# First-stage copies, banks and gates, latents in pairs, and two projections moved, in a one-core diffusion backbone

## The chip, the cores and the metric

The kernel runs on one core of one Trainium2 chip. The time is device microseconds (us) of one execution of the whole program. The core has a matrix engine (PE, TensorE), VectorE (DVE), ScalarE (ACT), GpSimd (POOL) and SyncE (SP), each with its own in-order queue. An instruction that waits holds up all that stand behind it on its engine. Results of PE go to PSUM, which has eight banks of 128 x 512 fp32. DMAs are issued here from SP's and from POOL's queue.

## The reference

One latent stream x (512 tokens, 1024 channels) goes through two layers. The change lies in the first: RMS norm with a shift and scale from the conditioning vector c (context tokens: from c_ctx), then multi-head latent attention over 256 context tokens and 512 latent ones.

```
m_lat = (silu_c @ ada_w[i] + ada_b[i]);  m_ctx = silu_cc @ ada_w[i] + ada_b[i]     # 6 x 1024 each
h_lat = rmsnorm(x, g) * (1 + sc_m) + sh_m          # h_ctx the same, from ctx and m_ctx
kv_a  = h @ wkv_a                                   # 256 latent + 64 rotary columns, 768 tokens
ckv   = rmsnorm(kv_a[..., :256]);  kv = ckv @ wkv_b # 8 heads, 128 key + 128 value columns
k     = rope(rmsnorm(concat(k_nope, k_pe)))
cq    = rmsnorm(h_lat @ wq_a)                       # 384 columns, 512 tokens
q     = rope(rmsnorm(cq @ wq_b))                    # 8 heads x 192
o     = softmax(q k^T * scale) v;  x = x + g_m * (o @ wo)
x     = x + g_f * (relu(modulate(x) @ w1) ** 2) @ w2
```

The second layer (gated mixing over positions, and another feed-forward) follows. Only the latent stream is returned.

## The kernel before

All data are fp32. A matrix product is made in three matmuls: each operand is split into a high part in fp32r and a low part that holds the rest, and high x high, high x low and low x high are added in PSUM (`mm3`, lines 80 to 82). The split of a weight is a cast on ScalarE (`split`, L72) and a subtraction on VectorE (L73), or with a scale L76. `Weights` loads a weight through SP's queue into one of four raw buffers and splits it; its high and low parts live in rings of five buffers in the first stage. A scheduler orders each engine's instructions by their place in the source, moved forward or back by what they need; `issue_after` puts an instruction behind another one of its engine.

The first stage has two pools of PSUM banks: `pt` with two and `pa` with six. It loads the tokens (`xn`), transposes them (`xct` for the context, `xt` for the latents) and spreads the inverse norms over partitions (`rp`, copied to `rsb`). Shift and scale of the first mixer come in four quarters of 256 channels. `ada_quarter(q)` loads four weights of 128 x 1024 (`ada<ch><q><i>`: ch 0 is the shift, 1 the scale), multiplies them with `c4` (silu of both conditioning vectors, high and low) in 32 matmuls into `ada_o`, copies the four rows to `adrow`, and turns them into columns `ada_c`, by matmuls with `sel`, which adds high and low. From the columns VectorE makes `bm` (shift) and `am` (scale). For each of eight channel tiles, `make_h` then forms `xa`, the high parts `ch`, `hh` on ScalarE and the low parts `cl`, `hl` on VectorE, and PE adds h times `wkv_a` into six accumulators `kva`, one for each tile of 128 tokens, which fill the six `pa` banks.

Behind that stand the latents. Each `kva` is normed (`kst`, with a power on GpSimd, L126), scaled to `ck`, transposed to `ckt` and split to `ckv_h`, `ckv_l`. In the same way `qa`, h times `wq_a` for one tile of tokens, becomes `cq`, `cqt`, `cq_h`, `cq_l`. `kv_proj(0)` makes keys and values of the first head, with a row of key norms `rkt`, `rr` that goes to DRAM and comes back over all partitions as `rk`. The rotary keys `krt` and `q_proj(0)` follow. In the attention `scores(h, half)` and `values(h, half)` go over eight heads in two halves of the tokens, with projections of later heads as fill between them. `scores` multiplies `s` by `rk` on VectorE (L638), so `rk` must be there.

In the background, `ada_step` makes the shifts, scales and gates of the other sublayers: GpSimd issues loads of `ada_w` (`adr`, 512 KB each, two buffers at first) and VectorE adds each to `acc`, eight to one row (L163, L165). These accs stand in VectorE's queue among the work of the latents.

## Time and profile before

| | us |
|---|---|
| median of 3 runs | 1386.79 (1385.57 to 1388.17) |
| profiled execution | 1386.22 |
| its span in the trace | 1384.4 |
| PE busy | 1335.3 (96%) |
| VectorE busy | 852.6 (62%) |
| ScalarE busy | 538.7 (39%) |
| GpSimd busy | 89.0 (6%) |

The span runs from the first to the last instruction of the trace; 1.8 us of the time lie around it. The mean clock granted to PE was 0.991 of full speed. The rows further down are from views of this one execution: a table of stretches of time, timelines of an engine (start, duration, engine, line, operation, output and inputs, shape, number, and in brackets how long the engine stood idle before and what ended that), groups of instructions, and DMA issues. A row with x12 stands for twelve instructions in succession.

### The profile page before, as it was taken

To read this page: it belongs to the slowest core of one execution; us is meant where nothing else is said; L and a number is where in the kernel's file an instruction comes from. 1 tells how busy PE (TensorE), PEld (TensorE's weight loads), DVE (VectorE), ACT (ScalarE), POOL (GpSimd) and SP (SyncE) were. 2 spreads that over 40 slices of the span, in tenths; PEclk is the share of its full clock that TensorE was granted. 3 is DMA by queue.
4 is the path that set the end of the run, shared out by engine and by line. 5 is a ranking of instruction groups with operands and counts; after the bars stand their busy time and mean duration, and the time that the engine had idled before them with its cause. 6 is when DMAs were issued, how large, how long until landed. Compare 5 with 4: busy or idle time off the path is not lost.

```text
span 1384.4 us, 18271 instructions
## 1 busy us (share of the span) xinstructions
PE 1335.3 (96%) x7071; PEld 1140.3 (82%) x7071; DVE 852.6 (62%) x1423; ACT 538.7 (39%) x1038; POOL 89.0 (6%) x140
## 2 busy tenths in 40 slices
PE   5988899999899999999999999999999999999998
PEld 4778889899888878888897888888888888888888
DVE  4877788887998888434466456555584344343452
ACT  6656556564641231422334323223254133241331
POOL 2031111110111111000000010000000000000000
PEclk8999999999999999999999999999999999999999
DMA  8551231321678886332323332222223223323311
GB/s 277 181 159 62 84 121 53 126 63 45 191 258 261 270 268 220 106 91 92 107 77 107 91 113 86 92 90 78 77 62 122 91 92 93 105 93 99 97 46 61
DMA packets 128070, 166.38 MB, mean 120 GB/s; under 512 B 7643, under 2 KB 111712, under 8 KB 127984
## 3 DMA queue, kind: packets, MB, share of 16 engines
q1 hardware_dynamic: 116032, 122.67, 28.1%
q0 software_dynamic: 11808, 42.03, 9.4%
q8 instruction: 55, 0.90, 0.3%
q10 hardware_dynamic: 144, 0.52, 0.1%
q14 instruction: 31, 0.25, 0.1%
HBM read 163.08 MB, written 2.12 MB: 119 GB/s over the span
## 4 chain that ended last, share of the span: by engine, by line
PE 78%; DVE 6%; DMA 5%; issue 5%; ACT 2%; POOL 1%; DVEq 0%; POOLq 0%; ACTq 0%
DMA adr<-in_ada_w_dram 5%; PE s L634 3%; PE v L80 2%; PE v L82 2%; PE v L81 2%; DVE acc L165 2%; PE f1d2o L80 1%; PE f1d0o L81 1%; PE f1d0o L82 1%; PE f1d0o L80 1%; PE f1d2o L81 1%; PE f1d2o L82 1%; PE f1d1o L80 1%; PE f0d2o L80 1%; PE f0d2o L81 1%
## 5 line engine op out<-in xcount | busy, mean ns | idle before, releaser
L165 DVE SCALAR_TENSOR_TENSOR acc<-adr,sil,acc 128x1024 f32<-128x1024 f32 x70 | 89.7, 1281 | 21.6 <-DMA adr<-in_ada_w_dram 21.4
L161 POOL DMA_DIRECT2D adr<-in_ada_w_dram x80 | 43.1, 539 | 223.9 <-DVE acc L165 129.5
L783 DVE TENSOR_TENSOR f1a<-f1a 128x512 f32<-128x512 f32 (+1 forms) x36 | 22.5, 629 | 38.1 <-ACT f1a L782 38.1
L72 ACT CAST f0uh<-f0a 128x512 fp32r<-128x512 f32 (+1 forms) x36 | 20.4, 572 | 53.3 <-DVE f0a L783 53.3
L638 DVE CUSTOM_DVE_ANT_0 p<-s,rk,rq 128x768 f32<-128x768 f32 x32 | 32.5, 1014 | 13.5 <-DMA rk<-rkd 9.2
L73 DVE TENSOR_TENSOR tl<-pt,th 128x512 fp32r<-128x512 f32 x48 | 32.0, 685 | 6.1 <-ACT th L72 5.9
L126 POOL TENSOR_TENSOR nst<-nst,mhalf 128x2 f32<-128x2 f32 x6 | 5.5, 919 | 455.9 <-DVE nst L125 455.9
L641 ACT ACTIVATE p<-p,sm 128x768 f32<-128x768 f32 x32 | 30.1, 941 | 12.1 <-DVE sm L640 12.1
L73 DVE TENSOR_TENSOR f1ul<-f1a,f1uh 128x512 fp32r<-128x512 f32 (+1 forms) x36 | 22.6, 632 | 19.7 <-ACT f1uh L72 19.5
L72 ACT CAST th<-pt 128x512 fp32r<-128x512 f32 x48 | 27.1, 587 | 18.8 <-PE o L82 12.6
L783 DVE TENSOR_TENSOR f0a<-f0a 128x512 f32<-128x512 f32 (+1 forms) x36 | 22.6, 627 | 18.1 <-ACT f0a L782 18.1
L72 ACT CAST f1uh<-f1a 128x512 fp32r<-128x512 f32 (+1 forms) x36 | 20.4, 572 | 32.8 <-DVE f1a L783 32.8
L73 DVE TENSOR_TENSOR f0ul<-f0a,f0uh 128x512 fp32r<-128x512 f32 (+1 forms) x36 | 22.5, 627 | 11.7 <-ACT f0uh L72 11.7
L80 PE MATMUL o<-th,vh 128*128 128x256 f32 x96 | 28.1, 293 | 0.7 <-ACT th L72 0.7
L81 PE MATMUL o<-tl,vh 128*128 128x256 f32 x96 | 28.3, 294 | 0.0
L601 DVE SCALAR_TENSOR_TENSOR xT<-wo,mod,xT 128x512 f32<-128x512 f32 (+1 forms) x40 | 25.1, 638 | 3.3 <-PE wo L82 3.0
L82 PE MATMUL o<-th,vl 128*128 128x256 f32 x96 | 27.1, 282 | 0.0
L656 PE MATMUL pt<-ident,p 128*128 128x128 f32 x192 | 26.8, 273 | 0.0
L893 DVE TENSOR_TENSOR gm<-gm,u 128x512 f32<-128x512 f32 x16 | 11.0, 689 | 20.6 <-ACT u L874 20.5
L656 PEld LDWEIGHTS pt<-ident,p 128*128 128x128 f32 x192 | 22.3, 141 | 1.0
L634 PE MATMUL s<-kh,qh 128*128 128x384 f32 x64 | 17.6, 357 | 4.3 <-DVE sm L638 4.2
L643 DVE TENSOR_SCALAR p<-p,sm 128x768 f32<-128x768 f32 x32 | 19.8, 618 | 0.6
(2637 smaller groups left out, 4622.8 us busy)
## 6 DMA issues: line engine op xcount, KB each, us to landing
adr<-in_ada_w_dram POOLq DMA_DIRECT2D x80, 512.0 KB, 4.8
rk<-rkd SPq DMA_DIRECT2D x8, 384.0 KB, 4.3
xn<-in_x_dram SPq DMA_DIRECT2D x4, 512.0 KB, 8.7
out_dram<-of SPq DMA_DIRECT2D x8, 256.0 KB, 2.1
xn<-in_ctx_dram SPq DMA_DIRECT2D x2, 512.0 KB, 3.6
ada000r<-in_ada_w_dram SPq DMA_DIRECT2D x1, 512.0 KB
ada001r<-in_ada_w_dram SPq DMA_DIRECT2D x1, 512.0 KB
ada100r<-in_ada_w_dram SPq DMA_DIRECT2D x1, 512.0 KB, 11.9
```

The source lines that it names most:

```text
L72: ACT.copy(out=hi, in_=src)
L73: eng.tensor_tensor(out=lo, in0=src, in1=hi.bitcast(F32), op=ALU.subtract)
L80: PE.matmul(o, lhsT=wh, rhs=mh, start=start, stop=False)
L81: PE.matmul(o, lhsT=wh, rhs=ml, start=False, stop=False)
L82: return PE.matmul(o, lhsT=wl, rhs=mh, start=False, stop=stop)
L161: nc.gpsimd.dma_start(out=r, in_=ada_w[l][k * P:(k + 1) * P, ch * D:(ch + 1) * D])
L165: DVE.scalar_tensor_tensor(out=acc, in0=r, scalar=sil[:, k, 0:1], in1=acc, op0=ALU.mult, op1=ALU.add)
L634: PE.matmul(S[:, n, :384], lhsT=a, rhs=b[:, n * 384:(n + 1) * 384], start=m == 0, stop=m == 4)
L638: DVE.tensor_tensor_reduce(out=e, in0=S[:, :, :384], in1=rk, op0=ALU.mult, op1=ALU.max, scale=rq, scalar=-3.0e38, accum_out=sm[:, 0:1])
L641: ACT.activation(out=e, in_=e, func=AF.Exp, bias=sm[:, 1:2], accum_out=sm[:, 2:3])
L656: PE.transpose(T[:, j, q * P:(q + 1) * P], Pr[h, 2 * half + q][:, (2 * jp + j) * P:(2 * jp + j + 1) * P], ident)
L783: DVE.tensor_tensor(out=f, in0=f, in1=f, op=ALU.mult)
```

## The change

In the first stage `t_c`, `t_cols` and `t_adab` take `pa` banks instead of `pt` banks, and the last two are issued behind the last transpose of x. The first quarter is written before `rp`, and `rp` is put behind its last matmul. One `adrow` copy takes both halves of `ada_o`. The columns come by four transposes, and a reduction on VectorE adds high and low (`adsum`). The scale half of a later quarter's splits is gated behind the `am` of the quarter before, and each quarter is written one ahead of its use, with the `wka` load first. The loads of cos, sin and of two gains stand behind the `wqa` loads in SP's queue. The latents go in pairs of token tiles: `ckv` in three, `cq` in two, with splits of 256 columns instead of 128. `query_latent(0)` is written before the norm of `kva`, in a `pt` bank. `kv_proj(1)` moves from behind the first scores into the latents.

```diff
-        t0 = pt("t_c")
+        t0 = pa("t_c")
-        t1 = pt("t_cols")
-        PE.transpose(t1[:, 16:87], rows, ident[:71, :71])
-        DVE.tensor_copy(out=cols[:, 16:87], in_=t1[:, 16:87])
-        t2 = pt("t_adab")
-        PE.transpose(t2[:, :96], arows, ident[:96, :96])
-        DVE.tensor_copy(out=adab, in_=t2[:, :96])
-        DVE.tensor_tensor(out=gqk, in0=cols[:, 53:54], in1=cols[:, 54:55], op=ALU.mult)
...
+        def ada_quarter(q, after=None, gate=None):
+
             row = inb.tile([4, 2, 256], F32, name="adrow", bufs=2)
             r = pt(f"ada_o{q}")
             for ch in range(2):
                 cs = slice(ch * 256, (ch + 1) * 256)
                 for i in range(2):
-                    wh, wl = W(ada_w[0], 4 * i, 4, ch * D + q * 256, 256, f"ada{ch}{q}{i}", POOL if SP[0] >> (2 * ch + i) & 1 else DVE)
+                    wh, wl = W(ada_w[0], 4 * i, 4, ch * D + q * 256, 256, f"ada{ch}{q}{i}", after=[gate] if gate and ch else ())
                     for k in range(4):
                         kk = 4 * i + k
-                        PE.matmul(r[:4, cs], lhsT=c4[:, kk, :], rhs=wh[:, k, :], start=kk == 0, stop=False)
-                        PE.matmul(r[:4, cs], lhsT=c4[:, kk, :], rhs=wl[:, k, :], start=False, stop=kk == KT - 1)
-                ACT.copy(out=row[:, ch, :], in_=r[:4, cs])
+                        with tc.issue_after(after) if after and kk == 0 else nullcontext():
+                            PE.matmul(r[:4, cs], lhsT=c4[:, kk, :], rhs=wh[:, k, :], start=kk == 0, stop=False)
+                        m = PE.matmul(r[:4, cs], lhsT=c4[:, kk, :], rhs=wl[:, k, :], start=False, stop=kk == KT - 1)
+            ACT.copy(out=row.rearrange("p c n -> p (c n)"), in_=r[:4, :])
+            o = pt(f"ada_c{q}")
             for ch in range(2):
                 for b in range(2):
-                    j = (2 * ch + b) * 2
-                    PE.matmul(o[:, j:j + 2], lhsT=row[:, ch, b * P:(b + 1) * P], rhs=sel, start=True, stop=True)
+                    j = (2 * ch + b) * 4
+                    PE.transpose(o[:, j:j + 4], row[:, ch, b * P:(b + 1) * P], ident[:4, :4])
             ks = slice(2 * q, 2 * q + 2)
-            o3 = o[:, :8].rearrange("p (c b j) -> p c b j", c=2, b=2)
+            sm = inb.tile([P, 4, 2], F32, name="adsum", bufs=2)
+            DVE.tensor_reduce(out=sm, in_=o[:, :16].rearrange("p (x s j) -> p x j s", x=4, s=2), axis=AX.X, op=ALU.add)
+            o3 = sm.rearrange("p (c b) j -> p c b j", c=2)
 
...
+            g = DVE.scalar_tensor_tensor(out=am[:, ks, :], in0=am[:, ks, :], scalar=1.0,
+                                         in1=bc(cols[:, G_MIX + 2 * q:G_MIX + 2 * q + 2]), op0=ALU.add, op1=ALU.mult)
+            return m.ins, g.ins
...
-                    PE.transpose(o[:, t * P:(t + 1) * P], xn[2 + t][:, k * P:(k + 1) * P], ident)
+                    last = PE.transpose(o[:, t * P:(t + 1) * P], xn[2 + t][:, k * P:(k + 1) * P], ident).ins
...
+        t1 = pa("t_cols")
+        with tc.issue_after(last):
+            PE.transpose(t1[:, 16:87], rows, ident[:71, :71])
+        DVE.tensor_copy(out=cols[:, 16:87], in_=t1[:, 16:87])
+        t2 = pa("t_adab")
+        with tc.issue_after(last):
+            PE.transpose(t2[:, :96], arows, ident[:96, :96])
+        DVE.tensor_copy(out=adab, in_=t2[:, :96])
+        DVE.tensor_tensor(out=gqk, in0=cols[:, 53:54], in1=cols[:, 54:55], op=ALU.mult)
+
+        m0, gate = ada_quarter(0, last)
         rp = [pa("rp0"), pa("rp1")]
         for t in range(NT):
             o = rp[0][:, t * P:(t + 1) * P] if t < 2 else rp[1][:, (t - 2) * P:(t - 1) * P]
-            PE.matmul(o, lhsT=rs6[:, t:t + 1].to_broadcast([P, P]), rhs=ident, start=True, stop=True)
+            with tc.issue_after(m0) if t == 0 else nullcontext():
+                PE.matmul(o, lhsT=rs6[:, t:t + 1].to_broadcast([P, P]), rhs=ident, start=True, stop=True)
...
             if k % 2 == 0:
-                ada_quarter(k // 2)
-                wkh, wkl = W(wkv_a, k, 2, 0, nka, f"wka{k}", POOL if SP[1] >> k & 1 else DVE)
+                wkh, wkl = W(wkv_a, k, 2, 0, nka, f"wka{k}")
+                if k < KT - 2:
+                    m0, gate = ada_quarter(k // 2 + 1, None, gate)
...
+        with tc.issue_after(bg_state["load"]):
+            nc.sync.dma_start(out=cosT, in_=rope_cos.rearrange("(t p) r -> p t r", p=P))
+            nc.sync.dma_start(out=sinT, in_=rope_sin.rearrange("(t p) r -> p t r", p=P))
+            nc.sync.dma_start(out=gq_b, in_=q_norm[:, NOPE:].to_broadcast([P, ROPE]))
+            nc.sync.dma_start(out=gk_b, in_=k_norm[:, NOPE:].to_broadcast([P, ROPE]))
...
-        for t in range(NT):
-            ck = wqp.tile([P, QL], F32, tag="ck", name="ck", bufs=3)[:, :KVL]
-            DVE.tensor_scalar(out=ck, in0=kva[t][:, :KVL], scalar1=st[:, 2:3], scalar2=None, op0=ALU.mult)
-            DVE.tensor_tensor(out=kg[:, t, :], in0=kva[t][:, KVL:nka], in1=gk_b, op=ALU.mult)
-            o = pt(f"ckt{t}")
-            for j in range(2):
-                PE.transpose(o[:, j * P:(j + 1) * P], ck[:, j * P:(j + 1) * P], ident)
...
-        kv0 = kv_proj(0)
-        for t in range(NL):
-            o = pa(f"qa{t}")
+        def query_latent(t):
+            o = qas[t] = (pa if t else pt)(f"qa{t}")
             for k in range(KT):
                 s = bass.ts(t, P)
                 mm3(o[:, :QL], hh[k][:, s], hl[k][:, s], wqa_h[:, k, :], wqa_l[:, k, :], k == 0, k == KT - 1)
-            if t >= QD:
-                latent_q(t - QD)
+            return o
+
+        query_latent(0)
+        for u in range(3):
+            st = ini.tile([P, 4, 2], F32, name="kst", bufs=3)
+            us = slice(2 * u, 2 * u + 2)
+            for j in range(2):
+                t = 2 * u + j
+                ACT.activation(out=junk[:, :KVL], in_=kva[t][:, :KVL], func=AF.Square, accum_out=st[:, 0, j:j + 1])
+                ACT.activation(out=junk[:, :ROPE], in_=kva[t][:, KVL:nka], func=AF.Square, accum_out=st[:, 1, j:j + 1])
+            rsq(st[:, 2, :], st[:, 0, :], 1.0 / KVL, EPS, st[:, 3, :])
+            DVE.tensor_scalar(out=epk[:, us], in0=st[:, 1, :], scalar1=1.0 / QK, scalar2=EPS, op0=ALU.mult, op1=ALU.add)
+            o = pt(f"ckt{u}").rearrange("p (k n) -> p k n", k=2)
+            for j in range(2):
+                t = 2 * u + j
+                ck = wqp.tile([P, QL], F32, tag="ck", name="ck", bufs=3)[:, :KVL]
+                DVE.tensor_scalar(out=ck, in0=kva[t][:, :KVL], scalar1=st[:, 2, j:j + 1], scalar2=None, op0=ALU.mult)
+                for k in range(2):
+                    PE.transpose(o[:, k, j * P:(j + 1) * P], ck[:, k * P:(k + 1) * P], ident)
+            s = slice(2 * u * P, (2 * u + 2) * P)
+            for k in range(2):
+                split(o[:, k, :], ckv_h[:, k, s], ckv_l[:, k, s], cols[:, G_KVA + k:G_KVA + k + 1])
+            for j in range(2):
+                DVE.tensor_tensor(out=kg[:, 2 * u + j, :], in0=kva[2 * u + j][:, KVL:nka], in1=gk_b, op=ALU.mult)
+        cqs = {}
+
+        def latent_q(u):
+
+            os_ = [pa(f"cqt{u}{i}").rearrange("p (k n) -> p k n", k=2) for i in range(2)]
+            for k in range(3):
+                for j in range(2):
+                    PE.transpose(os_[k // 2][:, k % 2, j * P:(j + 1) * P], cqs[2 * u + j][:, k * P:(k + 1) * P], ident)
+            s = slice(2 * u * P, (2 * u + 2) * P)
+            for k in range(3):
+                split(os_[k // 2][:, k % 2, :], cq_h[:, k, s], cq_l[:, k, s], cols[:, G_QA + k:G_QA + k + 1])
+
+        def rotary_keys(u):
+            o = pt(f"krt{u}")
+            for j in range(3):
+                PE.transpose(o[:, j * P:(j + 1) * P], kpe[:, 3 * u + j, :, :].rearrange("p a r -> p (a r)"), ident)
+            s = slice(u * 384, (u + 1) * 384)
+            ACT.copy(out=rh[:, s], in_=o[:, :384])
+            return DVE.tensor_tensor(out=rl[:, s], in0=o[:, :384], in1=rh[:, s].bitcast(F32), op=ALU.subtract).ins
+
+        kv0, kv1 = kv_proj(0), kv_proj(1)
+        ktmp = hp.tile([P, NT, ROPE], F32, tag="vl", bufs=3, name="ktmp")
+        for t in range(NL):
+            o = qas[t] if t in qas else query_latent(t)
             st = ini.tile([P, 4], F32, name="qst", bufs=4)
             ACT.activation(out=junk[:, :QL], in_=o[:, :QL], func=AF.Square, accum_out=st[:, 0:1])
             rsq(st[:, 2:3], st[:, 0:1], 1.0 / QL, EPS, st[:, 3:4])
             cqs[t] = wqp.tile([P, QL], F32, tag="ck", name="cq", bufs=3)
             DVE.tensor_scalar(out=cqs[t], in0=o[:, :QL], scalar1=st[:, 2:3], scalar2=None, op0=ALU.mult)
-        for t in range(NL - QD, NL):
-            if t >= KV:
+            if t == 1:
+                rope(DVE, kpe[:, :, 0:1, :], kg.unsqueeze(2), NT, 1, ktmp.unsqueeze(2), 0)
+                DVE.tensor_copy(out=kpe[:, :, 1, :], in_=kpe[:, :, 0, :])
                 drain(kv0, 1)
-            latent_q(t)
-        ktmp = hp.tile([P, NT, ROPE], F32, tag="vl", bufs=3, name="ktmp")
-        rope(DVE, kpe[:, :, 0:1, :], kg.unsqueeze(2), NT, 1, ktmp.unsqueeze(2), 0)
-        DVE.tensor_copy(out=kpe[:, :, 1, :], in_=kpe[:, :, 0, :])
-        for u in range(2):
-            o = pt(f"krt{u}")
-            for j in range(3):
-                PE.transpose(o[:, j * P:(j + 1) * P], kpe[:, 3 * u + j, :, :].rearrange("p a r -> p (a r)"), ident)
-            s = slice(u * 384, (u + 1) * 384)
-            ACT.copy(out=rh[:, s], in_=o[:, :384])
-            DVE.tensor_tensor(out=rl[:, s], in0=o[:, :384], in1=rh[:, s].bitcast(F32), op=ALU.subtract)
-
+            if t == 2:
+                latent_q(0)
+                drain(kv0, 1)
+        drain(kv0, 1)
+        rotary_keys(0)
+        rotary_keys(1)
+        drain(kv1, 1)
+        latent_q(1)
         drain(kv0)
+        drain(kv1)
 
 
 
@@ -692,7 +722,6 @@
...
         steps = [(h, half) for h in range(HEADS) for half in range(2)]
         scores(0, 0)
-        drain(kv_proj(1))
```

On PE, at the start of the first quarter, these rows stood after the last transpose of x (names: `rp` the spread norms, `t_cols` and `t_adab` the transposed gains and biases). Before:

```order
L428 MATMUL xt_259<-ident,xn_169 128x128
L436 MATMUL rp_266<-ident,rs_177 128x128 x2
L436 MATMUL rp_267<-ident,rs_177 128x128 x4
L366 MATMUL t_cols<-ident,rows 128x71
L369 MATMUL t_adab<-ident,arows 128x96
L389 MATMUL ada_o_278<-ada000h,c_82 4x256
L390 MATMUL ada_o_278<-ada000l,c_82 4x256
```

and after:

```order
L382 MATMUL ada_o_267<-ada000l,c_82 4x256
L381 MATMUL ada_o_267<-ada001h,c_82 4x256
L431 MATMUL t_cols<-ident,rows 128x71
L435 MATMUL t_adab<-ident,arows 128x96
L382 MATMUL ada_o_267<-ada001l,c_82 4x256
```

The quarter's matmuls now come first, with the two transposes among them. Its end, after the change:

```order
L381 MATMUL ada_o_267<-ada101h,c_82 4x256
L382 MATMUL ada_o_267<-ada101l,c_82 4x256
L444 MATMUL rp_335<-ident,rs_170 128x128 x2
L444 MATMUL rp_336<-ident,rs_170 128x128 x4
L388 MATMUL ada_c_325<-ident,adrow 128x4 x4
L381 MATMUL ada_o_352<-ada010h,c_82 4x256
```

`rp` has moved behind the whole quarter, and `ada_c` comes from transposes of `adrow`.

On VectorE, in the latents, where the accs and the latents share the queue. Before:

```order
L165 SCALAR_TENSOR_TENSOR acc_1351<-adr_1355,sil,acc_1351 128x1024
L125 TENSOR_SCALAR qst<-qst 128x1
L76 SCALAR_TENSOR_TENSOR ckv_l<-ckt_853,cols,ckv_h 128x128
L494 TENSOR_SCALAR ck<-kva_354,kst 128x256
L495 TENSOR_TENSOR kg<-kva_354,gk_b 128x64
L494 TENSOR_SCALAR ck<-kva_355,kst 128x256
L495 TENSOR_TENSOR kg<-kva_355,gk_b 128x64
L76 SCALAR_TENSOR_TENSOR ckv_l<-ckt_853,cols,ckv_h 128x128
L76 SCALAR_TENSOR_TENSOR ckv_l<-ckt_869,cols,ckv_h 128x128
L165 SCALAR_TENSOR_TENSOR acc_1351<-adr_1358,sil,acc_1351 128x1024
```

and after:

```order
L165 SCALAR_TENSOR_TENSOR acc_1405<-adr_1409,sil,acc_1405 128x1024
L125 TENSOR_SCALAR qst<-qst 128x1
L76 SCALAR_TENSOR_TENSOR ckv_l<-ckt_865,cols,ckv_h 128x256
L520 TENSOR_SCALAR ck<-kva_424,kst 128x256
L527 TENSOR_TENSOR kg<-kva_424,gk_b 128x64
L165 SCALAR_TENSOR_TENSOR acc_1405<-adr_1412,sil,acc_1405 128x1024
L125 TENSOR_SCALAR qst<-qst 128x1
L165 SCALAR_TENSOR_TENSOR acc_1405<-adr_1415,sil,acc_1405 128x1024
L520 TENSOR_SCALAR ck<-kva_425,kst 128x256
L527 TENSOR_TENSOR kg<-kva_425,gk_b 128x64
L556 TENSOR_SCALAR cq<-qa_830,qst 128x384
L76 SCALAR_TENSOR_TENSOR ckv_l<-ckt_888,cols,ckv_h 128x256
```

Between the `ck` of two neighbouring tiles now stand two accs where there was none, the first `cq` stands behind them (and behind one more acc ahead of these rows), and the splits have 256 columns.

On PE, at the end of the latents, before the first `q_proj(0)` matmul (`kt` are key transposes, `rkt` the key norms of a head). Before:

```order
L82 MATMUL kv_1165<-wkb0h,ckv_l 128x256
L535 MATMUL krt_1153<-ident,kpe 128x128 x3
L535 MATMUL krt_1159<-ident,kpe 128x128 x3
L266 MATMUL kt_1184<-ident,kn_1178 128x128 x2
L274 MATMUL rkt_1191<-ident,st_1079 6x128
L80 MATMUL q_1239<-wqb00h,cq_h 128x384
L81 MATMUL q_1239<-wqb00l,cq_h 128x384
```

and after:

```order
L82 MATMUL kv_1219<-wkb1h,ckv_l 128x256
L543 MATMUL krt_1134<-ident,kpe 128x128 x3
L266 MATMUL kt_1171<-ident,kn_1165 128x128 x2
L266 MATMUL kt_1171<-ident,kn_1209 128x128 x2
L274 MATMUL rkt_1190<-ident,st_982 6x128
L266 MATMUL kt_1238<-ident,kn_1232 128x128 x2
L274 MATMUL rkt_1245<-ident,st_1151 6x128
L80 MATMUL q_1293<-wqb00h,cq_h 128x384
L81 MATMUL q_1293<-wqb00l,cq_h 128x384
```

The second head's keys and values, with their `rkt`, now stand ahead of the query projection.

## Rows read from the trace of the kernel before

**Rows 1.** The page's busy times of the engines

```profile
PE 1335.3 (96%) x7071; PEld 1140.3 (82%) x7071; DVE 852.6 (62%) x1423; ACT 538.7 (39%) x1038; POOL 89.0 (6%) x140
```

**Rows 2.** Table of stretches: us, busy time (count) by engine, clock, DMA share, GB/s

```profile
0.00:22.80 22.80, 10.84 (x63) 8.45 (x64) 8.71 (x16) 16.60 (x28) 8.13 (x24) 1.00 0.88 284
22.80:74.70 51.90, 47.24 (x304) 37.84 (x304) 39.79 (x67) 28.66 (x47) 0.00 (x0) 0.90 0.59 182
74.70:112.20 37.50, 27.92 (x170) 26.36 (x170) 29.81 (x82) 20.33 (x80) 13.34 (x21) 0.95 0.53 165
112.20:200.00 87.80, 81.14 (x535) 75.97 (x536) 68.28 (x170) 53.96 (x165) 13.44 (x15) 0.98 0.29 89
200.00:1384.40 1184.40, 1168.14 (x6003) 991.66 (x6001) 706.02 (x1090) 419.17 (x720) 54.09 (x80) 1.00 0.36 115
```

**Rows 3.** PE's timeline of the first stage, start, us, instruction, idle before

```profile
22.82 0.33 PE L389 MATMUL ada_o<-ada000h,c 128*4 128x256 f32 x1 [4.25 <-DVE cols L367]
...
28.36 0.28 PE L389 MATMUL ada_o<-ada100h,c 128*4 128x256 f32 x1 [2.01 <-ACT adrow L391]
...
73.94 0.75 PE L82 MATMUL kva<-wka6h,hl 128*128 128x320 f32 x4
```

**Rows 4.** VectorE's timeline of the first stage

```profile
20.18 1.22 DVE L73 TENSOR_TENSOR ada100l<-ada100r,ada100h 128x1024 fp32r<-128x1024 f32 x1
...
33.49 0.48 DVE L447 SCALAR_TENSOR_TENSOR xa<-xcT,am,rsb 128x256 f32<-128x256 f32 x1
...
45.16 0.16 DVE L401 TENSOR_TENSOR bm<-ada_c,adab 128x4 f32<-128x4 f32 x1 [2.50 <-PE ada_c L395]
```

**Rows 5.** VectorE's busy time from first xa to last hl, one stretch

```profile
33.49:72.10 38.61, 33.51 (x56) 0.96 0.56 173
```

**Rows 6.** ScalarE's timeline of the first stage

```profile
27.00 1.04 ACT L72 CAST ada011h<-ada011r 128x1024 fp32r<-128x1024 f32 x1 [1.45 <-DMA ada011r<-in_ada_w_dram]
...
45.95 1.05 ACT L72 CAST ada121h<-ada121r 128x1024 fp32r<-128x1024 f32 x1 [4.49 <-PE kva L82]
```

**Rows 7.** PE's timeline of the latents, first ckt and first key norms

```profile
75.97 0.44 PE L498 MATMUL ckt<-ident,ck 128*128 128x128 f32 x2 [1.28 <-DVE ck L494]
...
112.16 0.38 PE L274 MATMUL rkt<-ident,st 128*6 128x128 f32 x1 [1.15 <-POOL st L272]
```

**Rows 8.** GpSimd's timeline, first background load after kva

```profile
75.62 1.17 POOL L161 DMA_DIRECT2D adr<-in_ada_w_dram  x2 [0.33 <-issue]
```

**Rows 9.** The page's DMA issues, the background loads

```profile
adr<-in_ada_w_dram POOLq DMA_DIRECT2D x80, 512.0 KB, 4.8
```

**Rows 10.** VectorE's timeline, last acc of the first eight

```profile
101.34 1.28 DVE L165 SCALAR_TENSOR_TENSOR acc<-adr,sil,acc 128x1024 f32<-128x1024 f32 x1 [1.00 <-DMA adr<-in_ada_w_dram]
```

**Rows 11.** VectorE's groups, 74.7 to 112.2: busy us, mean ns, idle before

```profile
L165 DVE SCALAR_TENSOR_TENSOR acc<-adr,sil,acc 128x1024 f32<-128x1024 f32 x7 | 9.0, 1283 | 5.4 <-DMA adr<-in_ada_w_dram 5.4
```

**Rows 12.** PE's timeline, head 1's projection and two rows of scores

```profile
126.21 0.28 PE L80 MATMUL kv<-wkb1h,ckv_h 128*128 128x256 f32 x1
...
127.63 0.58 PE L634 MATMUL s<-kh,qh 128*128 128x384 f32 x2
...
147.48 0.62 PE L634 MATMUL s<-kh,qh 128*128 128x384 f32 x2 [1.44 <-DVE sm L638]
```

**Rows 13.** VectorE's timeline, first softmax and second head's p

```profile
126.52 1.02 DVE L638 CUSTOM_DVE_ANT_0 p<-s,rk,rq 128x768 f32<-128x768 f32 x1 [0.42 <-PE s L634]
...
131.72 0.62 DVE L643 TENSOR_SCALAR p<-p,sm 128x768 f32<-128x768 f32 x1
...
146.40 1.02 DVE L638 CUSTOM_DVE_ANT_0 p<-s,rk,rq 128x768 f32<-128x768 f32 x1 [4.00 <-DMA rk<-rkd]
```

**Rows 14.** PE alone in one stretch: us, busy (count), clock, DMA share, GB/s

```profile
29.70:36.50 6.80, 6.56 (x31) 0.50 0.78 234
```

**Rows 15.** PE's timeline, transposes early and in the attention

```profile
6.51 2.82 PE L423 MATMUL xct<-ident,xn 128*128 128x128 f32 x12 [0.19 <-DMA xn<-in_ctx_dram]
...
139.85 1.04 PE L656 MATMUL pt<-ident,p 128*128 128x128 f32 x8
```

More of the change, by code (lines that the diff above doesn't have):

```diff
@@ L1 @@
-from contextlib import ExitStack, contextmanager
+from contextlib import ExitStack, contextmanager, nullcontext
 from types import SimpleNamespace
@@ L482, in hybrid_dit_kernel @@
         at.hp, at.W, at.pt, at.pm = hp, W, pt, pa
[L485 to L514 removed]
+        qas = {}
+        def query_latent(t):
+            o = qas[t] = (pa if t else pt)(f"qa{t}")
             for k in range(KT):
```

28 lines of the change are left out of this document (2 added, 26 removed).

## The prediction

> **What bounds the kernel now.** The page's list of engines comes first: PE is busy for 1335.3 of 1384.4 us [rows 1], so the end can only move by time in which PE stands still, or runs at the lower clock, or does less. The table by stretch tells where that is [rows 2]: span less PE's busy time is 12.0 us up to 22.8, 4.7 up to 74.7, 9.6 up to 112.2, 6.7 up to 200, and only 16.3 in the 1184.4 us behind. The change touches the first 160 us, so 32.9 us of standstill is what it can work on, and whatever it wins there arrives at the end unless the attention gives it back. The reader is then to see, in PE's timeline, two waits ahead of the first matrix's halves [rows 3], in VectorE's the operation from which the first stage is one long row of its work [rows 4, 5], in ScalarE's which load it stands for [rows 6], and behind the first stage a chain of loads that goes through VectorE's queue [rows 7 to 11].
>
> **The change part by part.** *First quarter, banks.* The first ada_o matmul starts at 22.82, 4.25 us after PE was ready, because cols' copy holds its bank and stands on VectorE behind four lo copies of 1.22 us; the second half waits 2.01 more for ScalarE to read the other half of the same bank [rows 3]. With t_c, t_cols and t_adab in the other pool, and one adrow copy for both halves, both waits have no reason left. The matmuls then follow the lo copies one by one, from about 18 us, and end soon after the last of them, near 24. But PE's gain of 5 to 6 us isn't the stage's: what opens the stage is the first xa on VectorE, at 33.49 [rows 4]. Ahead of it stand, in VectorE's new order, ada011l, a copy to rsb, the reduce, three small operations and ada110l; ada111l is now behind it. ada011l hangs on a load: ScalarE stood 1.45 us for ada011r, till 27.00 [rows 6], and its buffer had come free when ada100l ended, at 20.18 + 1.22 = 21.40 [rows 4], so 5.6 us passed between. The two rsb copies no longer stand ahead of ada100l, so it ends some 0.8 sooner: landing 26.2. Then 1.04 (hi), 1.22 (lo), about 0.7 for the copy of rsb (one and a half times xa's 0.48 [rows 4]), about 0.7 for the four small ones, 1.22 for ada110l: 31.1, less the overlap of neighbours, 30.5. If moving the four small loads off SP's queue brings ada011r 2 us sooner, it is 28.5; if the load takes 2 us longer, 32.5. I take **30.5, a lead of 3.0**.
>
> *From the first xa to the last hl.* That took 38.6 us, of which VectorE worked 33.5 [rows 5]. The change adds ada111l here (1.22) and three reduces. No row shows a reduce of this form; the nearest small one is 0.16, an upper end is 0.48 for 128x256 [rows 4]; I take 0.2 each, nearer the small one since it reads 16 columns. Sum 35.3. Of the 5.1 us of standstill, 2.50 is bm waiting for a quarter's columns [rows 4], which now come a quarter ahead; the 4.49 that ScalarE waits for wka0's buffer [rows 6] stays in part, since the extra weight load ahead only changes who asks for the buffer. I leave 1.5 us (0 to 5.1): 36.8. The last hl then ends at 67.3 instead of 72.1, **4.8 us sooner** (worst 32.5 + 40.4 = 72.9, best 28.5 + 35.2 = 63.7), and kva, which follows it [rows 3], near 69.9.
>
> *query_latent(0).* Its 24 matmuls of 384 columns move into this stage. At 0.118 us for 256 columns (12 kv matmuls between 126.21 and 127.63 [rows 12]) that is an estimate of 24 x 0.177 = 4.2 us. PE had 4.7 us idle in the stage [rows 2], and the stage begins earlier; it is hidden, and costs up to 4.2 if it isn't. It needs hh, hl and wqa, which come as the stage goes, and holds one of the two pt banks until its cq.
>
> *Pairs.* Twelve lo splits of 128 columns become six of 256, twice, and six rsq chains become three. In this stretch that makes VectorE's work a little less, while kv_proj(1)'s copies (vl three times, kl twice, wkb1l, some 3.3 us by the same operations later) come in; 29.8 of 37.5 us were busy [rows 2]. A pair's ck waits for two sums of squares and one pow, so the first ckt, which waited 1.28 us [rows 7], will wait about 3. I put the cost at nothing, because it isn't what ends last: adr loads do. The first is issued at 75.62, behind the last kva's pow [rows 8]; the last of its eight accs ends at 101.34 + 1.28 = 102.62 [rows 10]. That is 27.0 us with 5.4 us of VectorE waiting for the loads themselves [rows 11], each 4.8 us in flight [rows 9]. Then 9.5 us to the rkt transpose at 112.16 [rows 7], behind which q_proj begins. Nothing in the change shortens a load, so I move the chain as a whole: 70.8 + 27.0 + 9.5 = **107.3**, with the lead of 4.8 kept.
>
> *kv_proj(1).* Its 36 matmuls (36 x 0.118 = 4.2) and 7 transposes (0.1 each) leave the attention, where PE has no slack to speak of: 4.9 us. They enter a stretch where PE stands still for 9.6 us and which also loses 4.2 us of qa. Cover: these 13 us. So **4.9 us** come off, or nothing if the chain doesn't cover them.
>
> *Behind it.* VectorE waited 4.00 us and then PE 1.44 us for the second head's rk, a row that goes through DRAM [rows 12, 13]; its transpose now comes before q_proj, so 1.4 us go. On the other side kv1 stood between the first scores and the first value transposes, and covered the softmax: from 126.52 to the end of the first normalising at 132.3 are 5.8 us [rows 13], and what is left there (a third of kv_proj(2), four transposes of queries, the second scores) makes about 4.8 by its count; 1.0 us of new wait. Net **0.4**. The moved small loads of cos, sin and the two gains now land after wqa6 and are first needed by kg, behind ck: nothing, or if they come late something below the 4.00 us that rk's row costs now.
>
> **Sum**, against the profiled execution of 1386.2 us (span 1384.4, 1.8 around it; the median of the three runs is 0.6 above): 4.8 + 4.9 + 0.4 = 10.1, thus **1376**. The bounds of the first stage (-0.8 to 8.4), of query_latent (up to 4.2 lost) and of the last part (a loss of 1.0 to a gain of 1.4) make the range.
>
> **The rivals.** *PE becomes the bound of the first stage.* The granted clock was 0.50 in stretches behind the present waits, as from 29.70 to 36.50, where 31 matmuls took 6.56 us, twice their price [rows 14]. In the stage PE was busy 47.2 us; with qa's 4.2 it is 51.4 unless the waits' end also ends the low clock. In favour: twelve early transposes take 2.82 us, but eight later ones 1.04 [rows 15], and new transposes stand right ahead of the first quarter. Against: the stage's matmuls now follow each other sooner. If the clock stays low for ten more us, PE needs some 51 of the 52 us that it has, and the stage ends about 2 us later: **1378**, chance 0.12. The Trainium skill has a rule on this, in "TensorE: Matmul & The Clock Gate", section "Part 4: PE-mode transpose": the full clock doesn't engage for transposes. By that rule the case just priced would be the likely one; the early transposes agree with it and the later ones, at full pace, don't.
>
> *The attention takes filler back.* With kv1 gone, every later softmax could wait more. PE's 6.7 us of standstill from 112.2 to 200 [rows 2] is where it would grow. For: the order is otherwise the same from there, with a head's projection less in reserve. Against: fill work of heads 2 and 3 follows soon. At 4 us: **1380**, chance 0.14.
>
> *Slower: pairs behind the loads.* qa0 keeps a pt bank until its cq, and that cq and the later pairs' ck stand on VectorE behind up to four accs, each of which waits for a load of 4.8 us. If latents are served only link by link, q_proj's start is set by four serial links of issue 0.6, landing 4.8, acc 1.3 = 6.7 us. The end is later than now by more than 2.8 us only if q_proj starts beyond 112.2 + 5.3 + 2.8 = 120.3, that is 13.0 beyond my 107.3: four links 3.3 longer each, landings of 8.1 instead of 4.8. At that point **1389**, beyond it more. For: the DMA engines are already half busy there [rows 2], and wkb1's load joins. Against: the loads of the first 22.8 us moved 284 GB/s, here it was 165 [rows 2]. Chance 0.05.
>
> *The change doesn't reach the bound*, since ada011r or wka0's buffer sets the first stage as before and the lead is lost on VectorE, which is busiest from 112 on: 1386.2 - 1.4, about **1385**, chance 0.06. A first stage as good as its best bound gives **1370**, chance 0.07.
>
> **How the numbers follow.** My forecast has 0.56, between 1373 and 1378. The other gains (1378, 1380, 1370) have 0.33. About 0.2% or 2.8 us is what a measurement here can tell from no change: faster means below 1384.0. Faster is thus 0.56 + 0.33 = 0.89, less 0.01 for the upper tail of these: 0.88; same 0.07; slower 0.05. The range from 1370 to 1381 leaves out the last two rivals and half of the best case.
>
> **What would show it.** After: the first ada_o matmul near 18 rather than 22.82; first xa near 30.5; last kva near 70 with qa0's matmuls between; first ckt waiting about 3 us; eight accs still within about 27 us; q_proj from about 107; no wait for rk at the second head's p; standstill behind 200 us as before, 16. I am wrong if xa still starts past 33, if the accs' chain grows past 30, or if the waits for softmax in the first two heads grow by more than 2.

## The result, and the profile after

The changed kernel takes 1377.45 us (median of 4 runs, 1371.87 to 1378.22), the kernel before 1386.78. The ratio is 0.9932, with a 95% interval of 0.9910 to 0.9953: some 9.3 us sooner, where 1376 was forecast. The profiled execution is the fastest of the four (1371.87, span 1370.1), so one trace of it flatters the change by 5 to 6 us. A second trace of the same program, taken with the experiments (1377.59, span 1375.8), stands beside it below as *again*.

The table by stretch, in the same cuts as [rows 2], columns as there (behind the length: PE, its weight loads, VectorE, ScalarE, GpSimd):

```profile
0.00:22.80 22.80, 14.62 (x82) 11.33 (x83) 8.71 (x15) 16.60 (x28) 8.12 (x24) 0.93 0.83 278
22.80:74.70 51.90, 44.76 (x305) 38.44 (x303) 43.43 (x83) 34.30 (x67) 3.46 (x5) 0.95 0.71 218
74.70:112.20 37.50, 32.27 (x205) 30.85 (x203) 27.50 (x61) 19.40 (x74) 10.60 (x15) 0.89 0.48 145
112.20:200.00 87.80, 83.10 (x570) 78.55 (x569) 74.37 (x182) 55.37 (x164) 12.74 (x14) 1.00 0.28 86
200.00:1370.10 1170.10, 1155.64 (x5902) 978.82 (x5901) 696.40 (x1070) 410.80 (x693) 53.69 (x80) 1.00 0.36 116
```

PE stands still for 14.5 us behind 200 (16.3 before), so nearly all of the gain lies in the first 200 us, as forecast. PE's timeline of the first stage, which answers to [rows 3], and its end:

```profile
16.43 0.28 PE L381 MATMUL ada_o<-ada000h,c 128*4 128x256 f32 x1 [1.52 <-ACT ada000h L72]
17.69 0.28 PE L382 MATMUL ada_o<-ada000l,c 128*4 128x256 f32 x1 [0.98 <-DVE ada000l L73]
...
20.86 0.42 PE L381 MATMUL ada_o<-ada100h,c 128*4 128x256 f32 x1
...
68.33 0.75 PE L82 MATMUL kva<-wka6h,hl 128*128 128x320 f32 x4
```

Both waits of [rows 3] are gone; the first quarter's matmuls follow the copies one by one from 16.4. VectorE's timeline, which answers to [rows 4]: the small reduce, the first xa and the last hl,

```profile
28.28 0.17 DVE L391 TENSOR_REDUCE adsum<-ada_c 128x8 f32<-128x16 f32 x1
...
30.26 0.48 DVE L455 SCALAR_TENSOR_TENSOR xa<-xcT,am,rsb 128x256 f32<-128x256 f32 x1
...
64.25 0.75 DVE L457 SCALAR_TENSOR_TENSOR hl<-xa,bm,hh 128x512 fp32r<-128x512 f32 x1
```

and its busy time between them (columns as in [rows 5]):

```profile
30.26:65.00 34.74, 34.35 (x61) 0.98 0.73 216
```

VectorE now has 0.4 us of standstill there, where it had 5.1, so in this trace the first stage is VectorE's work almost alone. In *again* the same stretch is 36.6 us long with 2.2 of standstill, 2.1 of it waits for ScalarE's copies of `ada121` and `ada131`. Behind it, on PE, the first ckt and the start of q_proj ([rows 7]):

```profile
72.36 1.08 PE L522 MATMUL ckt<-ident,ck 128*128 128x128 f32 x4 [3.10 <-DVE ck L520]
...
106.53 0.38 PE L274 MATMUL rkt<-ident,st 128*6 128x128 f32 x1 [2.14 <-POOL st L272]
106.56 0.67 PE L80 MATMUL q<-wqb00h,cq_h 128*128 128x384 f32 x1
```

GpSimd's timeline has what I had not looked for, the first background loads ([rows 8]), and the power for which the last rkt waits:

```profile
63.45 1.16 POOL L161 DMA_DIRECT2D adr<-in_ada_w_dram  x2 [47.13 <-DVE cl L457]
...
105.15 1.33 POOL L272 TENSOR_TENSOR st<-st,mhalf 128x6 f32<-128x6 f32 x1 [4.53 <-DVE st L271]
```

Before, these two loads were issued at 75.62, behind the first power of kva's norm; now they stand ahead of it and go at 63.45. VectorE's eighth sum of the first row ([rows 10]):

```profile
94.07 1.27 DVE L165 SCALAR_TENSOR_TENSOR acc<-adr,sil,acc 128x1024 f32<-128x1024 f32 x1
```

So the chain is 31.9 us long (63.45 to 95.34), not 27.0, and ends 7.3 us sooner (in *again* 31.6 us and 5.2 sooner).

The best account is made from four landmarks on PE: the first ckt, the first q_proj matmul, the first matmul of the output projection (wo) and the first one with the second weight of the feed-forward (`f0u00w01h`, called f0 below; the first weight's matmuls start 6.3 to 7.1 us ahead of it in all runs). PE's busy time between them (us, busy with count, clock, DMA share, GB/s), before,

```profile
75.97:112.19 36.22, 27.91 (x169) 0.95 0.55 171
112.19:179.88 67.69, 62.55 (x419) 0.98 0.29 90
179.88:368.12 188.24, 181.15 (x1217) 0.98 0.28 90
```

and after, in the trace *again*:

```profile
74.22:108.61 34.39, 27.58 (x188) 0.98 0.52 155
108.61:168.47 59.86, 57.88 (x376) 0.96 0.29 90
168.47:359.94 191.47, 182.43 (x1216) 0.97 0.29 90
```

In the second trace the lead is 1.8 us at the first ckt, 3.6 at q_proj, 11.4 at wo, and 8.2 at f0, close to the 8.6 at the end. The first heads won 7.8, and 3.2 of that were given back behind them.

### The profile page after: what moved, and what is told of

It reads as the page before. It is cut to its first block, busy times and chain, and to the rows that moved or that the text cites. A ratio compares the mean times of both kernels' runs of the same rounds, so it can differ in the third digit from the quotient of the medians.

```text
span 1370.1 us, 18200 instructions
## 1 busy us (share of the span) xinstructions
PE 1330.4 (97%) x7055; PEld 1138.0 (83%) x7055; DVE 850.4 (62%) x1409; ACT 536.5 (39%) x1022; POOL 88.6 (6%) x137
## 4 chain that ended last, share of the span: by engine, by line
PE 85%; DVE 4%; issue 4%; DMA 3%; ACT 3%; POOL 0%; SPq 0%; DVEq 0%; ACTq 0%; POOLq 0%
PE s L664 3%; PE v L82 2%; PE v L80 2%; PE v L81 2%; DMA adr<-in_ada_w_dram 1%; PE f1d2o L80 1%; PE f1d0o L81 1%; PE f1d0o L80 1%; PE f1d0o L82 1%; PE f1d2o L81 1%; PE f1d2o L82 1%; PE f0d0o L80 1%; PE f0d1o L81 1%; PE f0d1o L80 1%; PE f0d1o L82 1%
## 5 line engine op out<-in xcount | busy, mean ns | idle before, releaser
L73 DVE TENSOR_TENSOR tl<-pt,th 128x512 fp32r<-128x512 f32 x48 | 31.9, 684 | 6.1 <-ACT th L72 5.8
L671 ACT ACTIVATE p<-p,sm 128x768 f32<-128x768 f32 x32 | 30.1, 941 | 13.3 <-DVE sm L670 13.3
## 6 DMA issues: line engine op xcount, KB each, us to landing
ada100r<-in_ada_w_dram SPq DMA_DIRECT2D x1, 512.0 KB, 11.4
```

The source lines that it names most:

```text
L73: eng.tensor_tensor(out=lo, in0=src, in1=hi.bitcast(F32), op=ALU.subtract)
L671: ACT.activation(out=e, in_=e, func=AF.Exp, bias=sm[:, 1:2], accum_out=sm[:, 2:3])
```

## The experiments

Each was timed in five rounds; the kernel before took 1385.3 to 1385.8 beside them. rk_late, no_adr, qa0_back and kv1_only ran on another chip than the other experiments; the kernel before took 1385.7 there, and 1385.75 and 1385.3 on the first chip. The table has the median, and from each one's trace the landmarks: start of the first ckt, and the lengths of the three stretches. Between the two traces of the changed kernel a length differs by up to 1.8 us and the start of the first ckt by 1.9.

| run | median us | first ckt | ckt to q_proj | q_proj to wo | wo to f0 |
|---|---|---|---|---|---|
| before | 1386.8 | 76.0 | 36.2 | 67.7 | 188.2 |
| changed (first trace) | 1377.5 | 72.4 | 34.2 | 59.2 | 189.7 |
| after_again | 1377.2 | 74.2 | 34.4 | 59.9 | 191.5 |
| first_old | 1382.4 | 78.7 | 34.2 | 60.2 | 191.5 |
| latents_old | 1379.6 | 71.8 | 36.0 | 68.1 | 188.9 |
| kv1_back | 1376.2 | 72.8 | 27.8 | 70.2 | 190.0 |
| kv1_only | 1384.8 | 76.5 | 41.4 | 59.4 | 191.5 |
| single_hoist | 1380.8 | 70.3 | 35.5 | 67.0 | 189.9 |
| qa0_back | 1378.0 | 74.3 | 35.9 | 59.9 | 192.1 |
| adr_behind | 1377.8 | 71.5 | 36.1 | 59.6 | 191.2 |
| no_adr | 1373.0 | 72.7 | 30.2 | 60.1 | 191.6 |
| before_no_adr | 1379.2 | 73.0 | 29.1 | 68.1 | 189.7 |
| rk_late | 1370.7 | 72.3 | 31.4 | 58.7 | 190.0 |
| adr_late | 1377.4 | 72.6 | 33.4 | 67.7 | 189.7 |

**after_again**, no edit.

> The changed kernel once more, unaltered, since its four times (1371.9, 1377.1, 1377.8, 1378.2 us) differ by more than those of before. If they come from two courses of one program, the profile and the times here fall at about 1372 or at 1377.5 with nothing between, and beside the first profile one place should show the 6 us. If it is a drift, they lie between.

Six runs gave 1374.63 to 1379.83, median 1377.17 (ratio 0.9934, 0.9917 to 0.9951). They lie between 1372 and 1377.5 and beyond: no two courses, but a spread. The two traces part step by step, 0.75 us at the first ada_c, 1.9 at the first ckt, 2.7 at wo, 4.4 at f0, 5.7 at the end. No single place holds it. The largest known part is VectorE's wait for two copies in the first stage, 2.1 us in the second trace and 0.2 in the first; what makes the rest was not settled.

**first_old and latents_old**, the two halves of the change: the first stage of before with the new latents, and the reverse.

The first, in the changed kernel, undoes all that stands ahead of `query_latent`:

```diff
-        t0 = pa("t_c")
+        t0 = pt("t_c")
...
-        m0, gate = ada_quarter(0, last)
...
-                if k < KT - 2:
-                    m0, gate = ada_quarter(k // 2 + 1, None, gate)
+                ada_quarter(k // 2)
...
```

> The first stage of before with the latents of the changed kernel (query_latent(0) ahead of kva's norm, pairs, the second head's projection moved). If the first stage's lead is passed on whole, this is 5 to 6 us slower than the changed kernel: the last hl near 72, q_proj near 112. Rival: the latents absorb it, as the background loads set their end and not the stage ahead of them; then it is less than 2 us slower.

The second undoes all from `query_latent` on:

```diff
-        query_latent(0)
-        for u in range(3):
+        for t in range(NT):
...
-        kv0, kv1 = kv_proj(0), kv_proj(1)
+        kv0 = kv_proj(0)
...
         scores(0, 0)
+        drain(kv_proj(1))
```

> The first stage of the changed kernel with the latents of before (single tiles, the first query matmuls behind the norms, the second head's projection behind the first scores). If the terms add, the end is 5 to 6 us sooner than before, and it and the run with the old first stage share the change's whole gain of 9 to 14 us between them. If the gain of one needs the other, both together fall short of it by 3 us or more.

With the old first stage the kernel takes 1382.38 (12 runs), 5.2 us more than the changed one, with the last hl at 72.3 and q_proj at 112.9, as expected. With the old latents it takes 1379.58, 6.2 us less than before. Thus the first stage brings 5 to 6 us and is passed on whole, and the rewritten latents bring 2 to 3.5 us. The halves add up (6.2 + 3.4 = 9.6 against 8.6).

**kv1_back and kv1_only**, the second head's projection put back, and moved alone.

In the changed kernel:

```diff
-        kv0, kv1 = kv_proj(0), kv_proj(1)
+        kv0 = kv_proj(0)
...
-        drain(kv1, 1)
...
-        drain(kv1)
...
         scores(0, 0)
+        drain(kv_proj(1))
```

> The changed kernel with the second head's projection back behind the first scores. If moving it gave 4.9 us of PE and the 1.4 us of rk's row, and if it cost nothing among the latents, this is 5 to 6 us slower than the changed kernel, with q_proj starting as early (106.6). Rival: the projection lengthens the latents, since its key norms stand ahead of q_proj on PE; then q_proj starts 3 to 4 us earlier here, near 103, and only about 2 us are lost at the end.

In the kernel before:

```diff
         drain(kv0)
+        drain(kv_proj(1))
...
         scores(0, 0)
-        drain(kv_proj(1))
```

> The kernel before with one edit, the second head's projection moved among the latents. If PE's standstill there (9.6 us) covers its 4.9 us, the end is 5 to 6 us sooner than before. If the projection's chain of splits, sums and power stands ahead of q_proj and delays it, q_proj starts some 3 us later and the end is 2 to 3 us sooner.

Putting it back costs nothing: 1376.22, 1.0 us below the changed kernel, within the spread. Moving it alone brings 1.0 us (1384.75, ratio 0.9993, 0.9979 to 1.0007), which the interval doesn't tell from nothing. The rival's mechanism holds in both, and is larger than was written: q_proj starts 6.0 to 8.0 us sooner with the projection put back, and 5.7 later with it moved alone. PE between the landmarks ckt, q_proj and wo, kv1_back first, then kv1_only:

```profile
72.75:100.58 27.83, 23.36 (x146) 0.96 0.61 182
100.58:170.80 70.22, 63.99 (x419) 0.94 0.29 86
```

```profile
76.46:117.85 41.39, 32.49 (x212) 0.97 0.52 163
117.85:177.23 59.38, 57.53 (x377) 0.96 0.27 86
```

Without the projection the new latents last 27.8 us, with it 34.4: it costs 6.6 there, and 5.2 in the old latents (36.2 to 41.4). In the heads it saves 10.4 and 8.3, of which 6.1 and 5.0 are PE's busy time and 4.3 and 3.3 its standstill. PE waited there behind the row of key norms, which is late where it follows the first scores (1.44 and 0.44 us before, 3.12 in kv1_back), and 1.9 us for the third head's power. VectorE's timeline of kv1_back:

```profile
135.67 1.02 DVE L666 CUSTOM_DVE_ANT_0 p<-s,rk,rq 128x768 f32<-128x768 f32 x1 [5.67 <-DMA rk<-rkd]
```

The standstill of the latents was not filled: in the old ones PE's busy time grew by 4.6 us and its standstill from 8.3 to 8.9, in the new ones by 4.2 and from 4.5 to 6.8. The projection makes new waits, as its tail stands ahead of q_proj on PE. PE's timeline of kv1_only, whose last rkt waits 3.08 us for the power on GpSimd while q_proj stands behind:

```profile
117.83 0.37 PE L274 MATMUL rkt<-ident,st 128*6 128x128 f32 x1 [3.08 <-POOL st L272]
117.85 0.67 PE L80 MATMUL q<-wqb00h,cq_h 128*128 128x384 f32 x1
```

**rk_late** moves that tail alone.

```diff
         drain(kv0)
-        drain(kv1)
+        drain(kv1, 2)
...
-        drain(q_proj(0)); ada_step(8)
+        drain(q_proj(0))
+        drain(kv1); ada_step(8)
```

> The changed kernel with the last step of the second head's projection, the transpose of its key norms and their way through DRAM, behind q_proj(0) instead of ahead of it. If PE's wait of 2.1 us for that power on GpSimd is what sets q_proj's start now, q_proj starts 2 to 3 us sooner, near 104, and the end is 2 to 3 us sooner than the changed kernel's. Rival: cq's low part or the query weights come at 106 anyway, or the second head's p then waits for rk; then nothing is gained.

It takes 1370.73 us (1367.86 to 1371.86; ratio to before 0.9888, 0.9868 to 0.9909), 6.4 less than after_again; the two intervals do not overlap, and so it beats both kernels. PE's timeline at the start of q_proj:

```profile
103.42 0.66 PE L266 MATMUL kt<-ident,kn 128*128 128x128 f32 x2 [0.88 <-ACT rr L276]
103.73 0.67 PE L80 MATMUL q<-wqb00h,cq_h 128*128 128x384 f32 x1
```

q_proj starts 2.8 us sooner than in the first trace of the changed kernel and 4.9 sooner than in the second; the wait of 2.1 to 2.4 for the power is gone, and the second head's p doesn't wait for rk. Against the second trace the landmarks show 3.0 of the gain in the latents, 1.2 in the heads and 1.5 behind them; 1.9 lies ahead of the first ckt, where the two programs don't differ, and belongs to the spread. So the moved tail is seen to bring some 3 us, as expected; for the rest of the 6.4 no cause was shown. The bulk of the projection, left in the latents, still costs 3.6 us there (31.4 against kv1_back's 27.8): PE's busy time is 5.0 longer, and only 1.4 of that came out of its standstill.

**single_hoist and qa0_back** part the pairs from the early query matmuls. single_hoist is latents_old with query_latent(0) alone moved ahead; qa0_back is the changed kernel with it moved back.

```diff
...
+        query_latent(0)
         kg = hp.tile([P, NT, ROPE], F32, tag="vh", bufs=3, name="kg")
...
```

> The run with the old latents (single tiles, the second head's projection behind the first scores, 1379.6 us), with query_latent(0) alone moved ahead of kva's norm. Beside kv1_back (1376.2, q_proj at 100.6) it lacks the pairs and what follows from them. If the pairs shorten the latents, q_proj starts at 104 or later. If the early query matmuls are what shortens them, q_proj starts near 101 and the end is within 1 us of kv1_back.

```diff
-            o = qas[t] = (pa if t else pt)(f"qa{t}")
+            o = qas[t] = pa(f"qa{t}")
...
-        query_latent(0)
```

> The changed kernel with query_latent(0) behind kva's norm, in a bank of the larger pool. Its 4.2 us of matmuls then leave the first stage, where they were said to be hidden. If the latents are bound by a chain and not by PE, nothing changes at the end (within 1 us), kva ends no earlier than 69 and the first wait for ckt grows. If PE's work binds the latents, q_proj starts up to 4 us later and so does the end.

Early query matmuls on single tiles bring nothing at the end (1380.75 against 1379.58). With pairs, undoing them costs 0.8 us at the end (1377.97) and 1.5 us in the latents, about the spread. But kv1_back, which differs from single_hoist by the pairs and by the order of the work that was written with them, has latents of 27.8 instead of 35.5 us and an end 4.5 us sooner. So the pairs, with that order, are what shortens the latents; the two were not parted. VectorE's busy time from the first ckt to q_proj shows how, kv1_back first, then single_hoist:

```profile
72.75:100.58 27.83, 24.09 (x57) 0.96 0.61 182
70.30:105.85 35.55, 29.50 (x79) 0.86 0.55 174
```

VectorE is busy for 5.4 us less, in 57 operations instead of 79 (2.3 us of it only moved out of the stretch: three splits of weights and one of the rotary keys), and stands still for 3.7 instead of 6.1. PE's timeline of single_hoist shows for what it waited, ckt after ckt:

```profile
81.65 0.44 PE L518 MATMUL ckt<-ident,ck 128*128 128x128 f32 x2 [2.29 <-DVE qst L125]
...
85.11 0.69 PE L518 MATMUL ckt<-ident,ck 128*128 128x128 f32 x2 [3.02 <-DVE ckv_l L76]
...
87.68 0.69 PE L518 MATMUL ckt<-ident,ck 128*128 128x128 f32 x2 [1.89 <-DVE cq L541]
```

VectorE's queue serves six tiles there; with pairs, only one later ckt waits, 0.7 us. These waits are not the length itself: latents_old has none of them and is as long (36.0), as PE does query matmuls in their place.

**no_adr, before_no_adr, adr_behind and adr_late** are on the background loads. The first two leave out seven of eight loads and sums of one row, from the changed kernel and from the kernel before.

```diff
-                nc.gpsimd.dma_start(out=r, in_=ada_w[l][k * P:(k + 1) * P, ch * D:(ch + 1) * D])
+                if n or not k:
+                    nc.gpsimd.dma_start(out=r, in_=ada_w[l][k * P:(k + 1) * P, ch * D:(ch + 1) * D])
+                if n == 0 and k:
+                    pass
-                if k == 0:
+                elif k == 0:
```

> The changed kernel without seven of the eight background loads and sums of the first row, which leaves that gate of the attention incomplete. By the prediction the chain of these loads sets the end of the latents: without it q_proj should start 8 us sooner or more, near 98. Rival: the latents are bound by PE, by the pairs' own chain and by the key norms ahead of q_proj; then q_proj starts 1 to 3 us sooner, no more than VectorE's freed 9 us let the copies come earlier.

> The kernel before without seven of the eight background loads and sums of the first row (that gate stays incomplete). The prediction moved the latents of before as a chain of these loads, 27.0 us plus 9.5 us behind. If that chain sets their end, q_proj starts 8 us sooner or more, near 104 instead of 112.2. Rival, as the same edit on the changed kernel showed: the loads are one burden of VectorE among others; q_proj starts 3 to 6 us sooner and the end is 3 to 5 us sooner.

adr_behind queues the loads behind the first power of kva's norm (`pw`) in the changed kernel:

```diff
...
-            rsq(st[:, 2, :], st[:, 0, :], 1.0 / KVL, EPS, st[:, 3, :])
+            pw = rsq(st[:, 2, :], st[:, 0, :], 1.0 / KVL, EPS, st[:, 3, :])
+            if u == 0:
+                bg_state["after"] = pw.ins
```

> The changed kernel with the first two background loads behind the first power of kva's norm on GpSimd, as in the kernel before, instead of ahead of it (they were issued at 63.5 us instead of 75.6). If the early issue is a gain of its own, the eight sums end some 4 us later and q_proj starts 1 to 4 us later, with the end as much later. If the sums don't bind, nothing changes within 1 us.

adr_late queues them in rk_late behind q_proj's last power (`at.pow`):

```diff
-            POOL.tensor_tensor(out=rq[:, us, :, 2], in0=rq[:, us, :, 1],
+            at.pow = POOL.tensor_tensor(out=rq[:, us, :, 2], in0=rq[:, us, :, 1],
...
-        drain(kv1); ada_step(8)
+        drain(kv1)
+        bg_state["after"] = at.pow.ins
+        ada_step(8)
```

> The version with the key norms behind q_proj (1370.7 us), and the background loads put behind q_proj's powers in GpSimd's queue, with all work done. If the loads only burden the latents, q_proj starts 3 to 4 us sooner than the 103.7 there and the end is 2 to 4 us sooner, near 1367.5. Rival: VectorE is as full behind q_proj (74 of 88 us) as among the latents, and the loads and sums slow the first heads by as much; then 1370 to 1373.

Without the row's loads the latents of before shrink by 7.1 us (36.2 to 29.1) and the end comes 6.1 sooner (1379.17); those of the changed kernel shrink by 4.0 to 4.2 (to 30.2), the end by 4.2 (1372.98). no_adr's q_proj comes 3.7 to 5.7 us sooner, between its two branches; before_no_adr's comes 10.1 sooner, but 3.0 of that lie ahead of the first ckt. So the loads with their sums did weigh on the latents of before, by most of the 8 us that the prediction's chain asks for, and weigh on them less now. The edit takes out VectorE's 9.0 us of sums together with the waits, so it doesn't tell a chain of loads from a burden of work. VectorE waits 2.5 us for the loads in the changed kernel where it waited 5.4 ([rows 11]); the same group after the change:

```profile
L165 DVE SCALAR_TENSOR_TENSOR acc<-adr,sil,acc 128x1024 f32<-128x1024 f32 x7 | 9.0, 1280 | 2.5 <-DMA adr<-in_ada_w_dram 2.5
```

Issuing the first two late again costs 1.8 us in the latents, where the sums then end 25.9 us behind the first ckt instead of 23.0 and 23.2, and 0.4 to 0.7 at the end (1377.84), which is within the spread. Putting them all behind q_proj is no gain: adr_late takes 1377.38, 6.6 more than the version that it started from and more than either branch had. PE's timeline in its first heads:

```profile
126.43 0.62 PE L664 MATMUL s<-kh,qh 128*128 128x384 f32 x2 [1.58 <-DVE sm L668]
130.45 1.01 PE L664 MATMUL s<-kh,qh 128*128 128x384 f32 x2 [1.25 <-DVE sm L668]
```

The sums now stand among the softmax's operations, and the stretch to wo lasts 67.7 us instead of 58.7. Its latents, with no loads in them, are not shorter (33.4 against 31.4). VectorE's busy time in them, and then PE's, show that the work of PE now fills them:

```profile
72.57:105.98 33.41, 20.11 (x59) 0.95 0.10 32
```

```profile
72.57:105.98 33.41, 28.78 (x188) 0.95 0.10 32
```

VectorE stands still for 13.3 us, 5.7 of it for ckt transposes on PE, and PE is busy for as long as in rk_late (28.8 against 28.4 us). So without the loads there was little left to win here; why the stretch is 2 us longer stays open.

## Why the prediction was right, and where it was not

**First stage: right.** The first xa came at 30.26 (30.73 *again*; 30.5 was said), the last hl ended at 65.0 and 67.3 (67.3 was said), the last kva group ends at 69.1 and 70.9 (near 70 was said). first_old prices it at 5.2 us against 4.8. Only the parts inside were a little off: VectorE's work was 34.4 in both rather than 35.3, and its standstill 0.4 and 2.2 rather than 1.5. The reduce took 0.17 us (0.2 was said).

**Latents: the right place by luck, from two errors of opposite sign.** q_proj was put at 107.3 and came at 106.6 and 108.6. But the step "I put the cost at nothing" for the pairs failed: with the order written with them they are a gain of 7.7 us in the latents (single_hoist to kv1_back), since fewer operations go through VectorE's queue. The loads, issued 12 us sooner, past the first power on GpSimd, have some 1.8 us of it (adr_behind). The chain of loads was not moved as a whole either: it grew to 31.9 and 31.6 us, past the 30 that was named as a sign of being wrong, and it no longer ends last, since 11.2 us lie between its end and q_proj instead of 9.5. I had taken the first load to follow "the last kva's pow"; the one ahead of it in [rows 8] was the first of six (at 74.73), and I had not looked at the new order of GpSimd's queue.

**kv_proj(1): the step that failed most.** Its "4.9 us come off, or nothing if the chain doesn't cover them" took the first branch. The runs show that in the latents it costs 5.2 (kv1_only) or 6.6 us (kv1_back), most of what the pairs had won. The sum of standstill, 9.6 us, was no cover: PE's standstill there did not shrink but grew, by 0.6 and 2.3 us. Of the 6.6 us, 3.0 go when the tail (PE to ScalarE to VectorE to GpSimd and back to PE) is moved behind q_proj, and 3.6 stay with the bulk (rk_late). Its gain in the heads was also mis-sized: 8.3 to 10.4 us instead of 4.9 + 0.4, with 3.3 to 4.3 us of standstill where I had taken the 1.44 of one wait. At the end it is worth 1.0 us alone, which the noise covers, and nothing in the changed kernel.

**The attention gives filler back: right as a rival, but not where it was put.** From wo to f0 every version with the projection moved takes 189.7 to 192.1 us and those with it in place 188.2 to 190.0. In *again* the loss is 3.2 us, where the rival had 4. The rival looked for it in PE's standstill from 112.2 to 200, and that fell, from 6.7 to 4.7 us in both traces. It is from wo to f0 that PE's standstill grew, from 7.1 to 9.0, and its busy time by 1.3; the waits for the softmax grew from 2.3 to 4.7. The largest of them on PE, before and then in *again*:

```profile
181.74 0.61 PE L634 MATMUL s<-kh,qh 128*128 128x384 f32 x2 [1.00 <-DVE sm L638]
```

```profile
172.05 1.01 PE L664 MATMUL s<-kh,qh 128*128 128x384 f32 x2 [2.68 <-DVE sm L668]
```

Of the 1.0 us of new wait that the forecast had at the first softmax little is there: PE's longest wait from 108.6 to 159.7 in *again* is one of 0.39 us.

**The other rivals.** PE did not become the bound of the first stage: the clock was low in two stretches of 3.4 and 3.3 us (below), and VectorE, with 0.4 us of standstill, did not wait for it. The serial links of the slower rival did not form, since q_proj started at 106.6 to 108.6, far from 120.3. The change did reach the bound of the first stage; the reason given for that rival, VectorE busiest from 112 on, misreads [rows 2], which has 81.14 us of PE there and 68.28 of VectorE. The first ckt's wait of 3.10 us was the 3 that was said, but it was not free: a lead of 5.6 us at kva's end became 3.6 at ckt.

Thus 10.1 us were forecast as 4.8 + 4.9 + 0.4. By place this came near: *again* has a lead of 3.6 us at q_proj (4.9 was said) and wins 4.6 from there to f0 (5.3 was said). By cause it did not: 5.2 us come from the first stage and 3.4 from the latents and heads together, in which pairs (a gain) and the projection (about nothing) have changed places.

## What to carry to other kernels

Standstill summed over a stretch is not room for more work: here 4.9 us of work filled none of 8.3 us in the old latents, and in the new ones, with its tail moved away, 1.4 of 4.5. Look at what the moved work's last instruction waits for, and at what stands behind it on that engine. When work is moved ahead of a stage, leave its last round trip behind the stage's first matmuls; here that was 3.0 us in the latents for a few lines, and the end came 6.4 sooner. And read the new order of every queue, GpSimd's too: a load that moves past one small operation starts a whole chain earlier.
